# Token mixers with the written order kept on three engines, and half a stream block between bursts of the chains

## The chip, the cores and the metric

The kernel runs on one core of one Trainium2 chip. The metric is device time in microseconds (us) of one execution; three runs of the kernel before gave 1572.19, 1572.81 and 1575.52, with a median of 1572.81.

## The reference

Two layers of a decoder trunk on 256 tokens of width 1024. A layer is four steps, each followed by a layer norm of (a times x plus the step's result): a SwiGLU block of width 2816, a step of three parallel token mixers, a second SwiGLU block, and a gated embedding. The change is in the mixer step:

```python
h  = x @ W_in        # columns split among RWKV-7, GLA, gated delta rule and merge gates
x  = LN(a*x + W_o(sum_b sigmoid(h_gate_b) * (Mixer_b(h_b) @ W_branch_b)))
```

RWKV-7 (8 heads of 64) and the gated delta rule (4 heads of 128) are recurrences that are computed in chunks of 64 or 128 tokens, each with the inverse of a triangular matrix; GLA (4 heads, keys of 64, values of 128) is a gated linear attention. Each mixer ends in a norm over its heads and a gate.

## The kernel before

**Tiling.** All 256 tokens are held on chip; activations lie with channels on the 128 partitions. Products of model width are made to nearly full precision out of three matmuls: an operand is split into a rounded part, `hi`, and the rest, `lo` (`split`, L313), and hi x hi, hi x lo and lo x hi are added up. Weights come from DRAM as units of 128 x 2048, in two halves of 128 x 1024: a DMA on the queue of SyncE (SP) brings a half into `raw` (four buffers), ScalarE (ACT) casts it to `hi`, VectorE (DVE) subtracts to get `lo` (four buffers each, `ahead`, L320). `unit` (L348) hands out the next unit in the order of `plan` (L67).

**The stream.** `stream` (L681) makes the columns of the combined projection, block by block in the order of `MIX` (L55). A block of 256 columns (`col_block`, L426, tile `cb`) is 2 x 24 matmuls of 128x256, 24 for each half of its columns, into one PSUM bank; ACT and DVE then take it out: a mix with the token before (`shift_mix`, L758), a convolution of four taps (`conv`, L765), a plain copy to DRAM for the merge gates (`put`, L773). C_R, C_K and C_V are RWKV's inputs, C_LQ and C_LV GLA's, C_DQ, C_DK and C_DV the delta rule's, each of two blocks; a pair (b, h) is half h of the merge gate of branch b; ("w", b, h) is the projection of branch b to half h (`project`, L1436, tile `pj`), which needs the whole branch. The last one is left to `merge` (L1479).

**The chains.** `rwkv` (L889), `gdn` (L1168) and `gla` (L1326) are generators, as `stream` is. What stands between two of a generator's yields is one burst: often a few matmuls, and the ACT and DVE work on their result. A chain's main parts are its gates and norms, products within chunks, the inverse (`inverse`, L784: a run of small DVE operations of growing size, then three rounds of matmuls), the steps from chunk to chunk and the norm at the end (`rwkv_out`, L1090; `rms_out`, L1121). GLA goes through seven levels of products (`LEVELS`, L59).

**What sets the order.** `mixers` (L670) takes a letter at a time from `ORDER` (L57): S, R, D or L lets the stream, RWKV, the delta rule or GLA run to its next yield. That is the order in which instructions are written down. It isn't the order in which they run: a scheduler orders each engine's instructions by readiness and priority while the program is built, with weight loads and their casts at high priority (L325), and the engines then keep that order. Only where `self.hold` is set does an instruction of PE, DVE or ACT keep its written place (`Engine`, L213, `pin`, L294): in `tok_pair`, the end of `ffn`, `merge` and `ple`, and here around eight matmuls of `gram` (L984 to 988).

**PSUM.** `ps` (L302) gives a tile a bank by a label: A has four, F and G two each; `TAGS` (L27) overrides the label written at the call.

Of the kernel before, what the change touches and what calls it, by code (L numbers as in the profile page):

```python
# [19 lines left out]
F32 = mybir.dt.float32  # L20
# [5 lines left out]
RAW, HL, N4, LEAD, FIN = 4, 4, 25, (3, 3), 1  # L26
TAGS = {"ab": "A", "gcol": "A", "gih": "G", "gks": "G", "ktr": "F", "lc": "F", "lo": "A", "misc": "G", "pa": "G", "pg": "G", "pj0": "A", "pj1": "A", "pq": "A", "pw": "G", "rih": "G", "st0": "A", "st1": "G", "un": "F"}  # L27
PJ = 0
MG = (4, 5)
MO = (3, 3)  # L30
P = 128
T = 256
NT = 2
# [201 lines left out]
class Trunk:  # L235
    def __init__(self, ctx, tc, I, out, dbg=None):
# [4 lines left out]
        self.halves = [(n, q) for n, u in enumerate(self.plan) for q in range(1 if u[0] == "fmisc" else 2)]  # L241
        self.at, self.used, self.ready, self.later, self.low, self.pending = 0, 0, [], [], [], ()
        self.branch = {}
        pool = lambda name, bufs, **kw: ctx.enter_context(tc.tile_pool(name=name, bufs=bufs, **kw))
# [103 lines left out]
    def unit(self, *key):  # L348

        assert self.plan[self.used] == key, (self.plan[self.used], key)  # L350
        self.used += 1
        self.subtract()
        n = 1 if key[0] == "fmisc" else 2
        self.ahead(n - len(self.ready))
        parts = [self.ready.pop(0) for _ in range(n)]

        def part(a, n):
            q, o = divmod(a, 1024)
            return parts[q][0][:, o:o + n], parts[q][1][:, o:o + n]

        return part
# [5 lines left out]

    def tok_unit(self, pss, unit, k0, start, stop, x=None):

        xh, xl = x or (self.xh, self.xl)  # L370
        for q in range(2):
# [298 lines left out]
    def mixers(self, i):  # L670

        self.got, self.branch, self.over = {}, {}, set()
        self.maker = {"b0": "R", "b1": "L", "b2": "D"}
        self.threads = {"S": self.stream(i), "R": self.rwkv(i), "D": self.gdn(i), "L": self.gla(i)}
        for name in ORDER + "RDLS":
            self.step(name)
        for name in "RDLS":
            while name not in self.over:
                self.step(name)

    def stream(self, i):  # L681

        nc = self.nc
        A = nc.scalar
        ps = self.col_block(self.unit("fwa", i))
        wa = self.pt.tile([P, T], F32, tag="wa", name="wa", bufs=1)
# [10 lines left out]
        self.shift_mix(mx, ps[:, :T], 14)  # L697
        ab = self.pt.tile([P, NT, 8], F32, tag="ab", name="ab", bufs=1)
        ps = self.ps("ab", "G")
        for t in range(NT):  # L700
            nc.tensor.transpose(ps[:, 8 * t:8 * t + 8], mx[64:72, t * P:t * P + P], self.ident[64:72, 64:72])
        A.copy(ab[:, :, 0:4], ps[:, :16].rearrange("p (t c) -> p t c", c=8)[:, :, 0:4])
        A.activation(ab[:, :, 4:8], ps[:, :16].rearrange("p (t c) -> p t c", c=8)[:, :, 4:8], AF.Sigmoid)
# [3 lines left out]
        self.got["misc"] = gl, ab  # L707
        yield
        for item in MIX:
            if isinstance(item, tuple) and item[0] == "w":  # L710
                yield "b%d" % item[1]
                self.project(i, *item[1:])
                if item != MIX[-1]:
                    yield
            elif isinstance(item, tuple):
                d = self.pd.tile([P, D], F32, tag="gd", name="gd", bufs=8)
                for u in range(2):
                    ps = self.col_block(self.unit("fcol", i, C_MG + item[0] * D + item[1] * 512 + 256 * u))
                    self.put(ps, d, u, AF.Copy)
# [3 lines left out]
            elif item == C_LV:  # L723
                pss = [self.ps(f"st{t}", "F") for t in range(NT)]
                for u in range(2):
                    self.tok_unit(pss, self.unit("tok", i, item, u), 4 * u, u == 0, u == 1)
                    if u == 0:
                        yield
                vt = self.s4("lv").rearrange("p (t c) -> p t c", t=2)
# [4 lines left out]
            elif item == C_LQ:  # L734
                qk = self.s4("lqk")
                q, k = qk[:, :512], qk[:, 512:]
                A.activation(q, self.col_block(self.unit("fcol", i, C_LQ)), AF.Identity, scale=0.125)
                yield
                A.copy(k, self.col_block(self.unit("fcol", i, C_LK)))
                self.got[item] = q, k  # L740
                yield
            else:
                out = self.s4("c%d" % item)
                for u in range(2):
                    ps = self.col_block(self.unit("fcol", i, item + 256 * u))
                    for c in range(2):
# [142 lines left out]
    def rwkv(self, i):  # L889
# [200 lines left out]
    def rwkv_out(self, t, y, bv, gl):  # L1090
# [59 lines left out]
    def unit_norms(self, xs):  # L1150
# [3 lines left out]
        for x, _ in xs:  # L1154
            sq = self.s4("usq")
            nc.scalar.activation(sq, x, AF.Square)
            sqs.append(sq)
        for sq in sqs:
            for q in range(2):
                ps = self.ps("un", "G")  # L1160
                s = slice(q * 512, q * 512 + 512)
# [6 lines left out]
    def gdn(self, i):  # L1168
# [10 lines left out]
        yield "misc"  # L1179
        ab = self.got["misc"][1]  # L1180
        e, s, s2, q, x = (small(n) for n in ("e", "s", "s2", "q", "x"))
# [21 lines left out]
        tri = kc[:, K_INCL:K_INCL + P]  # L1203
        pg = self.ps("gcol", "G")
        self.mm(pg[:, :8], tri, x.rearrange("p t h -> p (t h)"))
# [9 lines left out]
        for t in range(NT):  # L1215
            grow = self.ps("grow", "G").rearrange("p (h c) -> p h c", c=P)
            for h in range(4):
# [12 lines left out]
        k, q = self.got[C_DK], self.got[C_DQ]  # L1230
        self.unit_norms([(k, 1.0), (q, float(P) ** -0.5)])
        yield
# [6 lines left out]
        for t in range(NT):  # L1239
            pk, pq = self.ps("pk", "G"), self.ps("pq", "G")  # L1240
            for h in range(4):
# [52 lines left out]
        for t in range(NT):  # L1294
# [11 lines left out]
            V.tensor_tensor(out=vn, in0=pv, in1=self.head_bc(beta[:, t], P), op=ALU.mult)  # L1306
            yield
            if not t:
                vd = h3(self.s2("gvd"))
                V.tensor_tensor(out=vd, in0=vn, in1=self.head_bc(ec, P), op=ALU.mult)  # L1310
                pd = h3(self.ps("gd"))
# [3 lines left out]
                yield  # L1315
            ops = self.ps("go")
# [9 lines left out]
    def gla(self, i):  # L1326
# [48 lines left out]

        lw = None
        for n, s in enumerate(LEVELS):
            v5 = lambda ap: ap.rearrange("p (m f s) -> p m f s", f=2, s=s)
            if n % 2 == 0:
# [12 lines left out]
            V.tensor_tensor(out=v5(w)[:, :, 1], in0=v5(w)[:, :, 1], in1=v5(q)[:, :, 1], op=ALU.mult)  # L1392
            grams(w, w, 1 + n, s)
            yield
        grams(k, q, 0, 0)
        yield

# [11 lines left out]
        V.tensor_tensor(out=w4[:, :, 0:2], in0=w4[:, :, 0:2], in1=k4[:, :, 0:2], op=ALU.mult)  # L1409
        V.tensor_tensor(out=w4[:, :, 2:4], in0=w4[:, :, 2:4], in1=q4[:, :, 2:4], op=ALU.mult)  # L1410
        cross = self.s4("lcross").rearrange("p (a c) -> p a c", c=P)
        pss = [self.ps("lc", "G") for _ in range(2)]
# [23 lines left out]
    def project(self, i, b, h):  # L1436
# [39 lines left out]
        half(0)  # L1476
        half(1)

# [185 lines left out]
```

## Time and profile before

| | us |
|---|---|
| median of three runs | 1572.81 |
| the profiled execution | 1568.71 |
| its span, first to last instruction | 1566.9 |
| PE / DVE / ACT / POOL busy | 1494.9 / 1058.5 / 873.3 / 49.1 |
| mean granted clock of PE, share of full speed | 0.981 |

PE is TensorE, POOL is GpSimd. Spans are counted from the first instruction. Matmuls are pipelined, so a matmul's counted time overlaps that of its successor, and a busy PE isn't a PE at its peak. In the rows, `out<-in` are tiles by the program's names (`cb` a block's bank, `pj` a projection's, `hi` and `lo` weights, `lw`, `latt` and `lg` GLA's, `rig`, `riab`, `riof` the inverse of RWKV, `sq` and `kk` its keys), then come the shapes, a count, the busy time and the mean length of one in ns, and after the second bar the idle time of the engine just before, with what ended it.

### The profile page before, as it was taken

What the parts mean: (1) busy time and instruction counts of PE and PEld (TensorE: products, weight loads), DVE (VectorE), ACT (ScalarE), POOL (GpSimd) and SP (SyncE); (2) the same over time, 40 slices, a digit from 0 to 9 for tenths busy, and PEclk for the clock granted to TensorE, in tenths of its full rate; (3) what the DMA queues carried; (4) which work ended last, traced back from release to release, by engine and by line L of the source; (5) the groups of instructions that cost most, each with busy time, mean ns of one, the idle gap of its engine ahead of it and who ended that gap; (6) DMA issues with size and microseconds to landing.
All of it is one profiled execution on the core that took longest, in us unless ns stands there. A gap on an engine that the chain in (4) does not pass through costs nothing. (4 is left out here: it accounts for less than half of the span.)

```text
span 1566.9 us, 27601 instructions
## 1 busy us (share of the span) xinstructions
PE 1494.9 (95%) x11280; PEld 1356.7 (87%) x11280; DVE 1058.5 (68%) x1597; ACT 873.3 (56%) x1229; POOL 49.1 (3%) x85
## 2 busy tenths in 40 slices
PE   8999999988998999999999999998989889999997
PEld 7999889887987989998789997897979879899986
DVE  5555757787975875556865557577789658745567
ACT  5544558856654554445654445587665555644453
POOL 0000000000002000000000000000000020000001
PEclk9999999989999999999999999999999999999999
DMA  7765655532424655656555666554425256656562
GB/s 257 264 215 189 216 190 161 169 127 80 151 84 168 233 184 177 223 189 216 177 180 192 216 189 194 195 170 153 136 75 156 82 200 219 188 170 222 189 217 81
DMA packets 79775, 277.96 MB, mean 177 GB/s; under 512 B 9376, under 2 KB 9760, under 8 KB 79648
## 3 DMA queue, kind: packets, MB, share of 16 engines
q1 hardware_dynamic: 75744, 262.76, 51.8%
q0 software_dynamic: 3616, 13.11, 2.2%
q8 instruction: 88, 1.44, 0.4%
q10 hardware_dynamic: 288, 0.33, 0.1%
q14 instruction: 39, 0.32, 0.1%
HBM read 264.63 MB, written 11.53 MB: 176 GB/s over the span
## 5 line engine op out<-in xcount | busy, mean ns | idle before, releaser
L223 DVE TENSOR_TENSOR lo<-raw,hi 128x1024 fp32r<-128x1024 f32 (+1 forms) x459 | 555.4, 1220 | 316.1 <-ACT hi L223 313.7
L223 ACT CAST hi<-raw 128x1024 fp32r<-128x1024 f32 (+1 forms) x459 | 474.9, 1047 | 430.1 <-PE h L223 144.1
L223 PE MATMUL h<-xh,hi 128*128 128x256 f32 x1088 | 306.2, 282 | 5.9 <-ACT hi L223 5.5
L223 PE MATMUL h<-xl,hi 128*128 128x256 f32 x1088 | 305.8, 281 | 0.8 <-DVE xl L223 0.8
L223 PE MATMUL h<-xh,lo 128*128 128x256 f32 x1088 | 305.4, 281 | 0.0
L223 PE MATMUL cb<-xh,hi 128*128 128x256 f32 x864 | 247.1, 286 | 14.4 <-DVE c L223 11.1
L223 PE MATMUL cb<-xl,hi 128*128 128x256 f32 x864 | 244.5, 283 | 0.0
L223 PE MATMUL cb<-xh,lo 128*128 128x256 f32 x864 | 243.4, 282 | 0.0
L223 PEld LDWEIGHTS h<-xh,hi 128*128 128x128 f32 x1088 | 204.9, 189 | 7.3 <-ACT hi L223 5.5
L223 PEld LDWEIGHTS h<-xh,lo 128*128 128x128 f32 x1088 | 208.6, 192 | 0.1
L223 PEld LDWEIGHTS h<-xl,hi 128*128 128x128 f32 x1088 | 205.1, 189 | 2.2 <-DVE xl L223 1.0
L223 PEld LDWEIGHTS cb<-xh,hi 128*128 128x128 f32 x864 | 164.7, 191 | 18.8 <-DVE c L223 11.3
L223 PEld LDWEIGHTS cb<-xl,hi 128*128 128x128 f32 x864 | 164.8, 191 | 2.4 <-issue 1.0
L223 PEld LDWEIGHTS cb<-xh,lo 128*128 128x128 f32 x864 | 164.7, 191 | 1.9 <-issue 1.0
L223 PE MATMUL y<-hi,gh 128*128 128x512 f32 x352 | 137.8, 391 | 0.0
L223 PE MATMUL y<-lo,gh 128*128 128x512 f32 x352 | 137.1, 389 | 0.0
L223 PE MATMUL y<-hi,gl 128*128 128x512 f32 x352 | 136.2, 390 | 0.3 <-DVE gl L223 0.3
L223 PE MATMUL tb<-hi,xl 128*128 128x512 f32 x224 | 87.6, 391 | 2.1 <-DVE xl L223 2.1
L223 PE MATMUL tb<-hi,xh 128*128 128x512 f32 x224 | 88.5, 395 | 0.0
L223 PE MATMUL tb<-lo,xh 128*128 128x512 f32 x224 | 88.0, 393 | 0.0
L223 PEld LDWEIGHTS y<-hi,gl 128*128 128x128 f32 x352 | 66.1, 188 | 14.7 <-DVE gl L223 0.8
L223 PEld LDWEIGHTS y<-lo,gh 128*128 128x128 f32 x352 | 66.1, 188 | 12.2
(354 smaller groups left out, 2264.0 us busy)
## 6 DMA issues: line engine op xcount, KB each, us to landing
raw<-in_ws_dram SPq DMA_DIRECT2D x457, 512.0 KB, 4.4
gb<-in_ln_dram SPq DMA_DIRECT2D x16, 512.0 KB, 6.1
gd<-sg SPq DMA_DIRECT2D x32, 256.0 KB, 4.2
sgate<-gd POOLq DMA_DIRECT2D x12, 512.0 KB, 5.8
xd<-x POOLq DMA_DIRECT2D x4, 512.0 KB, 5.8
x<-xd POOLq DMA_DIRECT2D x4, 512.0 KB, 9.0
sw<-in_sw_dram SPq DMA_DIRECT2D x2, 768.0 KB, 8.7
xt<-in_xt_dram SPq DMA_DIRECT2D x4, 256.0 KB, 5.4
```

The costliest lines, as they stand in the source:

```text
L223: ins = f(*args, **kw)
```

## The change

`mixers` sets `self.hold` for the whole step, so that every instruction of PE, DVE and ACT keeps its written place there, and a new flag, `eager`, with which `unit` at once loads, casts and subtracts the next unit. The stream yields after half a block. `MIX` and `ORDER` are new: R's keys come first, GLA's inputs earlier, the projections of GLA stand before the last two gate blocks. The chains get a few yields more, so that a matmul and the ACT work that it needs lie in two bursts; GLA's products come one level later than the work that feeds them; two transposes move from the stream to the delta rule; tiles of PSUM get other labels. The instructions are the same.

```diff
-TAGS = {"ab": "A", "gcol": "A", "gih": "G", "gks": "G", "ktr": "F", "lc": "F", "lo": "A", "misc": "G", "pa": "G", ...
+TAGS = {"gk": "G", "lc": "G", "lg": "G", "lo": "G", "misc": "F", "pg": "G", "pj0": "F", "pj1": "F", "st0": "F", "st1": "F",
+        "tp": "G"}
...
-MIX = (C_R, C_K, C_DK, C_LV, (0, 0), C_V, C_LQ, (0, 1), C_DQ, (2, 0), (1, 1), C_DV, (2, 1), (1, 0), ("w", 0, 0),
-       ("w", 1, 1), ("w", 0, 1), ("w", 1, 0), ("w", 2, 0), ("w", 2, 1))
-ORDER = ("RRSRSSSDSSRSRRSSSRRRRRRRRRRSSRSRRRSDRRRRRSRSRDRRRRRRRRDRDSDRLDRRDRDLRDDSDSSSLDLDRLRDRRRDRDDRRRDLRLDD"
-         "SDDDDSDLLSDDDLLRDLSDLLRRLLDSSDSDSLLSSSSDSLDS")
+MIX = (C_K, C_R, (2, 0), C_LQ, (2, 1), C_DK, C_DQ, (1, 0), C_V, C_LV, (1, 1), C_DV, ("w", 1, 0), ("w", 1, 1), (0, 0), (0, 1),
+       ("w", 0, 0), ("w", 0, 1), ("w", 2, 0), ("w", 2, 1))
+ORDER = ("SSSRRSRDLSSDSRSSRSRSRSRSRSSRSRSRSSLSRSLSRSLSRLSRSRLSRSRLSRSRSRDSSSRSRSRDLSSRRSRDLRSRDLRSDLSRDLRS"
+         "DSDLLSRDLRSDLLLSRDLSRDSRDLSRDSRDRSRDSRDSRDRRSRDSRDRRSDSRSRDRSRDDSRDSRDDSRDSRDRDSDSDSSSS")
...
     def unit(self, *key):
         parts = [self.ready.pop(0) for _ in range(n)]
+        if self.eager:
+            self.ahead(2 - len(self.ready))
...
     def col_block(self, unit):
             for k in range(8):
                 self.col_mm(ps[:, c * T:c * T + T], unit, k, c)
+            if not c:
+                yield
...
     def mixers(self, i):
+        self.hold = self.eager = True
         for name in ORDER + "RDLS":
             self.step(name)
...
+        self.hold = self.eager = False
...
     def rwkv(self, i):
         A.activation(sq, kk, AF.Square)
+        yield
...
-                self.hold = True
                 for n in range(4):
...
-                self.hold = False
...
     def gla(self, i):
         for n, s in enumerate(LEVELS):
+            if n:
+                grams(*last)
...
-            grams(w, w, 1 + n, s)
+            last = w, w, 1 + n, s
             yield
+        grams(*last)
+        yield
...
     def project(self, i, b, h):
         half(0)
+        yield
         half(1)
```

More yields of the same kind stand before the norm's matmul in `rwkv_out` and `unit_norms`, before GLA's cross term (`lc`), in the value block of the stream (four parts in place of two) and in the delta rule's first state step, where one yield goes.

## Rows read from the trace of the kernel before

**Rows 1.** Head and first section of the page: span, and busy time by engine
```profile
span 1566.9 us, 27601 instructions
...
PE 1494.9 (95%) x11280; PEld 1356.7 (87%) x11280; DVE 1058.5 (68%) x1597; ACT 873.3 (56%) x1229; POOL 49.1 (3%) x85
```

**Rows 2.** Table of stretches: both mixer stages; columns as in the first line
```profile
core 0: us, PE busy (x) PEld busy (x) DVE busy (x) ACT busy (x) POOL busy (x), PEclk, DMA share, GB/s
...
217.00:501.40 284.40, 261.08 (x2545) 238.43 (x2543) 213.54 (x399) 187.84 (x282) 10.06 (x19) 0.96 0.41 132
...
996.40:1280.40 284.00, 258.39 (x2541) 236.00 (x2539) 213.04 (x398) 187.88 (x282) 9.28 (x17) 0.97 0.41 132
```

**Rows 3.** Table of stretches of 20 us, layer 0, same columns
```profile
300.00:320.00 20.00, 12.64 (x106) 10.98 (x105) 19.59 (x35) 8.70 (x18) 0.00 (x0) 0.81 0.32 105
...
480.00:500.00 20.00, 14.63 (x150) 13.52 (x149) 11.08 (x24) 12.31 (x16) 3.11 (x4) 1.00 0.41 143
```

**Rows 4.** Timeline of TensorE: start, length, instruction; then tile pj's own stretch
```profile
389.61 0.28 PE L223 MATMUL cb<-xh,lo 128*128 128x256 f32 x1
...
390.29 0.28 PE L223 MATMUL cb<-xh,lo 128*128 128x256 f32 x1
...
501.41 0.79 PE L223 MATMUL pj<-bh,hi 128*128 128x256 f32 x2 [6.02 <-ACT bh L223]
...
507.09 0.28 PE L223 MATMUL pj<-bh,lo 128*128 128x256 f32 x1
...
507.21 0.28 PE L223 MATMUL pj<-bh,hi 128*128 128x256 f32 x1
...
501.40:507.00 5.60, 4.23 (x18) 4.01 (x19) 0.00 (x0) 0.50 0.77 277
```

**Rows 5.** Groups of ScalarE instructions, shapes apart, 217 to 501 us
```profile
L223 ACT CAST hi<-raw 128x1024 fp32r<-128x1024 f32 x59 | 61.0, 1049 | 43.6 <-PE cb L223 37.4 <-issue 4.7 <-DMA raw<-in_ws_dram 1.0
...
L223 ACT ACT_TABLE_LOAD x21 | 26.9, 1283 | 1.2 <-DVE c L223 0.8
...
L223 ACT ACTIVATE c<-cb,om 128x256 f32<-128x256 f32 x12 | 5.5, 474 | 4.0 <-DVE c L223 3.9
...
L223 ACT ACTIVATE sq<-av,om,cv 128x256 f32<-128x256 f32 x4 | 2.2, 593 | 0.0
```

**Rows 6.** Groups of VectorE instructions, 217 to 501 us
```profile
L223 DVE TENSOR_TENSOR lo<-raw,hi 128x1024 fp32r<-128x1024 f32 x60 | 72.5, 1219 | 22.5 <-ACT hi L223 21.6 <-PE cb L223 0.3
...
L223 DVE SCALAR_TENSOR_TENSOR c<-cb,cv,c 128x255 f32<-128x255 f32 (+2 forms) x48 | 22.7, 477 | 2.5 <-ACT c L223 1.9
...
L223 DVE COPY_PREDICATED latt<-masks,lg 128x256 f32<-128x256 uint8 (+1 forms) x16 | 7.9, 553 | 2.2 <-PE lg L223 2.2
...
L223 DVE TENSOR_TENSOR lw<-lw,lqk 128x256 f32<-128x256 f32 x16 | 6.1, 421 | 0.0
...
L223 DVE TENSOR_TENSOR rig<-gram,kc 32x256 f32<-32x256 f32 x8 | 4.7, 590 | 0.1
```

**Rows 7.** Timeline of ScalarE around one change of table
```profile
267.19 0.69 ACT L223 ACTIVATE sq<-l,eps 128x512 f32<-128x512 f32 x1 [0.17 <-PE l L223]
...
267.90 1.28 ACT L223 ACT_TABLE_LOAD   x1
...
269.20 1.06 ACT L223 ACTIVATE sq<-sq 128x1024 f32<-128x1024 f32 x1
```

**Rows 8.** Timeline of VectorE inside the inverse of RWKV, layer 0
```profile
318.87 0.70 DVE L223 STREAM_TRANSPOSE rigt<-rig 128x512 f32<-128x512 f32 x1
...
323.49 0.22 DVE L223 TENSOR_REDUCE riab<-rigt 128x8 f32<-128x64 f32 x1
...
327.41 2.35 DVE L223 TENSOR_TENSOR riof<-gram,kc 128x1024 f32<-128x1024 f32 x2
```

**Rows 9.** Waits of the DMA issuing queue SP, 217 to 545 us; page's DMA issues
```profile
SPq L329 <- DVE lo L223: 217.5, 59, 27.4
...
sgate<-gd POOLq DMA_DIRECT2D x12, 512.0 KB, 5.8
```

More of the change, by code (lines that the diff above doesn't have):

```diff
@@ L242, in __init__ @@
         self.at, self.used, self.ready, self.later, self.low, self.pending = 0, 0, [], [], [], ()
+        self.eager = False
         self.branch = {}
@@ L366, in mm3, with tok_unit @@
         self.mm(out, ll, rh, False, stop)
-    def tok_unit(self, pss, unit, k0, start, stop, x=None):
+    def tok_unit(self, pss, unit, k0, start, stop, x=None, qs=range(2)):
         xh, xl = x or (self.xh, self.xl)
-        for q in range(2):
+        for q in qs:
             for t in range(NT):
@@ L684, in stream @@
         A = nc.scalar
-        ps = self.col_block(self.unit("fwa", i))
+        ps = yield from self.col_block(self.unit("fwa", i))
         wa = self.pt.tile([P, T], F32, tag="wa", name="wa", bufs=1)
@@ L697, in stream @@
         self.shift_mix(mx, ps[:, :T], 14)
[L698 to L703, printed above, removed]
         nc.gpsimd.memset(gl[:, 1:], 0.0)
@@ L706, in stream @@
         A.copy(gl[32:48, 2], mx[32:48])
-        self.got["misc"] = gl, ab
+        self.got["misc"] = gl, mx
         yield
@@ L711, in stream @@
                 yield "b%d" % item[1]
-                self.project(i, *item[1:])
+                yield from self.project(i, *item[1:])
                 if item != MIX[-1]:
@@ L717, in stream @@
                 for u in range(2):
-                    ps = self.col_block(self.unit("fcol", i, C_MG + item[0] * D + item[1] * 512 + 256 * u))
+                    ps = yield from self.col_block(self.unit("fcol", i, C_MG + item[0] * D + item[1] * 512 + 256 * u))
                     self.put(ps, d, u, AF.Copy)
@@ L725, in stream @@
                 for u in range(2):
-                    self.tok_unit(pss, self.unit("tok", i, item, u), 4 * u, u == 0, u == 1)
-                    if u == 0:
-                        yield
+                    un = self.unit("tok", i, item, u)
+                    for q in range(2):
+                        self.tok_unit(pss, un, 4 * u, u == 0, u == 1, qs=(q,))
+                        if (u, q) != (1, 1):
+                            yield
                 vt = self.s4("lv").rearrange("p (t c) -> p t c", t=2)
@@ L736, in stream @@
                 q, k = qk[:, :512], qk[:, 512:]
-                A.activation(q, self.col_block(self.unit("fcol", i, C_LQ)), AF.Identity, scale=0.125)
+                ps = yield from self.col_block(self.unit("fcol", i, C_LQ))
+                A.activation(q, ps, AF.Identity, scale=0.125)
                 yield
-                A.copy(k, self.col_block(self.unit("fcol", i, C_LK)))
+                ps = yield from self.col_block(self.unit("fcol", i, C_LK))
+                A.copy(k, ps)
                 self.got[item] = q, k
@@ L744, in stream @@
                 for u in range(2):
-                    ps = self.col_block(self.unit("fcol", i, item + 256 * u))
+                    ps = yield from self.col_block(self.unit("fcol", i, item + 256 * u))
                     for c in range(2):
@@ L1157, in unit_norms @@
             sqs.append(sq)
+        yield
         for sq in sqs:
             for q in range(2):
-                ps = self.ps("un", "G")
+                ps = self.ps("un")
                 s = slice(q * 512, q * 512 + 512)
@@ L1179, in gdn @@
         yield "misc"
-        ab = self.got["misc"][1]
+        mx = self.got["misc"][1]
+        ab = self.pt.tile([P, NT, 8], F32, tag="ab", name="ab", bufs=1)
+        ps = self.ps("ab")
+        for t in range(NT):
+            nc.tensor.transpose(ps[:, 8 * t:8 * t + 8], mx[64:72, t * P:t * P + P], self.ident[64:72, 64:72])
+        A.copy(ab[:, :, 0:4], ps[:, :16].rearrange("p (t c) -> p t c", c=8)[:, :, 0:4])
+        A.activation(ab[:, :, 4:8], ps[:, :16].rearrange("p (t c) -> p t c", c=8)[:, :, 4:8], AF.Sigmoid)
         e, s, s2, q, x = (small(n) for n in ("e", "s", "s2", "q", "x"))
@@ L1203, in gdn @@
         tri = kc[:, K_INCL:K_INCL + P]
[L1204 removed]
+        pg = self.ps("gcol")
         self.mm(pg[:, :8], tri, x.rearrange("p t h -> p (t h)"))
@@ L1230, in gdn @@
         k, q = self.got[C_DK], self.got[C_DQ]
-        self.unit_norms([(k, 1.0), (q, float(P) ** -0.5)])
+        yield from self.unit_norms([(k, 1.0), (q, float(P) ** -0.5)])
         yield
@@ L1310, in gdn @@
                 V.tensor_tensor(out=vd, in0=vn, in1=self.head_bc(ec, P), op=ALU.mult)
+            yield
+            if not t:
                 pd = h3(self.ps("gd"))
@@ L1374, in grams @@
                     "p (a b s) -> p a b s", a=4, s=out.shape[3]))
-        lw = None
+        lw = last = None
         for n, s in enumerate(LEVELS):
+            if n:
+                grams(*last)
             v5 = lambda ap: ap.rearrange("p (m f s) -> p m f s", f=2, s=s)
@@ L1476, in project @@
         half(0)
+        yield
         half(1)
```

10 lines of the change are left out of this document (4 added, 6 removed).

## The prediction

> **What bounds the kernel now.** I read the head of the page first: the span is 1566.9 us and PE counts as busy for 95% of it [rows 1]. Its profiled execution took 1568.7, 1.8 around the span. The three runs have a median of 1572.8, 4.1 above it; I sum against the profile and add 4.1 at the end.
>
> The change touches the mixers alone, once a layer. The table of stretches, cut from the first matmul of the first block to the first of a branch projection, gives 284.4 in layer 0 and 284.0 in layer 1, with PE busy 261.1 and 258.4, DVE 213.5, ACT 187.8 [rows 2]. So PE visibly idles for 23.3 in layer 0, in a few places: 7.4 of it in one 20 us slice where DVE is busy 19.6 and the granted clock falls to 0.81, 5.4 in the last slice, where the chains run out [rows 3]. After that the projections stand alone: the first waits 6.0 for ACT and starts at half clock, 18 matmuls in 5.6 us, then one each 0.12 [rows 4]. Five of the six projections (240 matmuls; the sixth belongs to the merge) take 5.6 + 222 x 0.12 = 32.2. **The stage with its five projections is 284.4 + 32.2 = 316.6 us**; that is the number to beat, twice.
>
> Busy PE hides waits. A block's matmuls start every 0.113 us (0.68 for six) but each counts 0.28 [rows 4], so a wait under 0.17 is not seen as idle.
>
> **What the change does, part by part.** It takes nothing out and adds nothing but order: 54 half blocks, 59 bursts of R, 34 of D, 20 of L, the same instructions. PE's own work, with no wait: a half block is 24 x 0.114 = 2.73; 54 of them are 147.4, the small block and the value block 14, five projections 28.8. The chains' bursts I take at 75, from the spacing of their matmuls; they lie between that and 261.1 - 161 = 100, which busy time leaves and which holds the hidden waits. Sum 265.3. So the waits of PE in the new order may come to 316.6 - 265.3 = **51.3 a layer before the kernel is slower**.
>
> Removed: the scheduler's choice on PE, DVE and ACT. Today it can put a weight subtraction of 1.22 [rows 6] between any two operations of a chain, once its cast is there. Added: each engine takes its instructions as written. A block's weights are cast on ACT (2 x 1.05) and subtracted on DVE (2 x 1.22) one block ahead, at the head of the block before [rows 5, 6]. The cover is that block, 2 x 2.73 = 5.5 of PE, and any chain work that ACT or DVE has in front of the casts eats it: 5.5 - 2.1 - 1.2 leaves 2.2. I walked the new order slot by slot: an engine starts an instruction when it is free and the last input is there, durations from the groups, two in a row overlapping by about 0.09 (two products of 1.22 in 2.35 [rows 8]), 0.05 allowed for a hand-over. The waits of PE that come out, per layer:
>
> - **Opening, 25.7**: the decay projection behind seven ACT steps 3.6, the cumulative gate 1.5, R0 3.3, the l2 sum behind ACT's copies 4.5, R1 2.5, (2,0)1 6.1, LQ 3.4, (2,1)0 0.9. One in full, (2,0)1: after the casts of the block before, ACT has a table load 1.28, an exponential 1.06, a wait for a DVE product 1.22, four scalings of 0.59, R1's two copies 0.95, three exponentials 3.18, then its casts 2.10 and the subtraction 1.22 [rows 5 to 7]: 13.4. PE has left of R1 and both halves of (2,0)0 7.3. Wait 6.1.
> - **Middle, 24.4**: DQ0 0.5, a GLA level 1.9, DQ1 3.1, (1,0)0 8.7, (1,0)1 6.2, the inverse's product 3.2, the cross term 0.9. In full, (1,0)0, on DVE: four mask products 0.59, a GLA step of two predicated copies 0.53 and four of 0.42 with ACT's exponential between them 0.7, six convolution taps 0.48, the first part of the inverse from 318.87 to 323.71 = 4.84, two subtractions 2.44 [rows 6, 8]: 15.8, less 1.6 of overlap, 14.2, against 5.5 of PE. Wait 8.7.
> - **Late, 13.8**: GLA's transposes behind DVE 3.9, (1,1)0 and (1,1)1 2.8, the delta inverse 3.5, the state steps of RWKV 3.6 in four.
> - **End, 5.9**: the branch b0 behind its norm, 5.5, where the present kernel waits 6.0, and b2 0.3.
>
> Sum 69.8; 59.8 of it in fifteen waits of 1.9 or more. The ten small ones (10.0) sit within the error of walking whole bursts, where an instruction may need only the first matmul: from 0 to 10.0, and I take half. **Stage 265.3 + 64.8 = 330.1, 13.5 longer; two layers 27.0; 1568.7 + 27.0 = 1595.7, and 4.1 for the median: 1599.8.**
>
> Edits at nothing: the transposes of a and b move to D and stay two; the GLA products move one level later; new yields issue nothing. New bank labels: any wait of that kind today is inside PE's 23.3 of idle time; from 0 to that, taken 0, since the stream keeps two banks and R and D four. SP: its weight loads lose their priority but wait 217 us for free buffers now [rows 9], and four buffers hold two blocks; taken 0. POOL: gates come back in 5.8 [rows 9], and in order ACT's sigmoid in front of the next casts would wait for that; from 0 (POOL ran ahead) to 5 x (5.8 - 2.2) = 18 a layer, taken 0 because POOL is busy 10 of 284 [rows 2]. Clock: a slice in which it fell shows 0.81 [rows 3], 0.19 x 20 = 3.8 of full speed lost. The walk has ten waits over 3, today's stage some four falls; from 0 to 6 x 3.8 = 23, taken 0 because the waits are spread out between dense blocks.
>
> Table loads: I count 20 changes of function set against 21 [rows 5]. Between the logarithm's end at 267.88 and the exponential's start at 269.20 lies the load of 1.28 and 0.04 more [rows 7], so a change costs 1.3. The Trainium skill, "ScalarE: Activation LUTs", section "What ACT_TABLE_LOAD costs", adds a drain of about 1.38 to each load; the trace does not show one. By the page six loads in the opening would add an estimated 8.3 a layer to ACT there, and the sum would be some 1616; as no row shows the drain, this gets no chance of its own.
>
> **Rivals.** *Faster: the casts are not late.* Its place is the queue of ACT and DVE in front of the stream's own blocks: ten of the waits (R0, R1, (2,0)1, LQ, (2,1)0, DQ0, DQ1, (1,0)0, (1,0)1, (1,1)1) are casts that stand behind bursts, 36.5 a layer. If bursts are shorter than I charge them, these go, the stage is 265.3 + 33.3 = 298.6, 18.0 shorter, and the time 1572.8 - 36 = 1537. It decides where 18.5 of the 36.5 go (13.5 if half the small waits go too). For it: ACT now idles 37.4 before casts, waiting only for PE to free a buffer [rows 5], so capacity is there, and the order has empty slots after heavy bursts. Against it: that idle time is spread over the stage, and the opening's ACT steps are long ones in a row.
>
> *No change: about half of them go*, waits near 51.3, within 1.6 a layer. The present kernel hides some 24.6 (261.1 - 236.5) behind busy matmuls and idles 23.3, so a trade of one kind of wait for another is possible. That the order is the old one in effect is excluded: blocks and projections change places.
>
> *Slower by more: the clock and the gates.* Ten waits over 3 us pull the clock down as they do now, 23, or ACT waits for gates, 18, a layer. With half of both, 41 over two layers, the time is 1600 + 41 = 1641. For it: PE's slices with 12.6 of 20 busy run at 0.81 [rows 3]. Against: most waits end within one block's length.
>
> **How the numbers follow.** The forecast, slower by one to three per cent, gets 0.57: the opening and the middle are sums of long instructions that must pass one queue. Faster gets 0.25, since the walk is coarse and its margin, 13.5 of 330, is small; no change 0.08; slower by more 0.10. Faster or slower by 0.2%, 3.1 us, is about what a measurement of this kernel tells from no change. The forecast's own range is 1590 (no small wait) to 1625 (all waits, 1610, and a third of the clock's bound, 15). The range for eight in ten goes from 1548, which leaves out about half of the faster case, to 1628, which leaves out most of the last one.
>
> **What would show it.** Right: DVE and ACT alternate in bursts, the group of casts shows idle before cb blocks on PE released by DVE lo, 25 or so in the first 90 us of a stage and again around the first inverse; the 6.0 before the projections stays near 5.5, and stage and projections take about 330. Wrong: PE idle below 23 a stage and hardly any before cb released by lo (the casts are on time, the faster rival); or slices at 0.8 clock in many more places (the third); or ACT waiting for the DMA of sgate. The forecast falls as a whole if ACT's casts stand ahead of bursts that are written before them.

## The result, and the profile after

The changed kernel takes **1690.74 us** (median of four executions, 1688.28 to 1693.27) against 1572.94 for the kernel before beside it: a ratio of **1.0746, with an interval of 1.0725 to 1.0767**. That is 118 us slower; forecast were 27, and the upper end of the range was 1628.

First the head of the page after, then its table of stretches: from the first block to the first projection in both layers, and, in layer 0, on to the end of the fifth projection.

```profile
span 1688.1 us, 27535 instructions
...
PE 1534.0 (91%) x11280; PEld 1387.5 (82%) x11280; DVE 1068.6 (63%) x1597; ACT 859.3 (51%) x1220; POOL 49.2 (3%) x85
```
```profile
core 0: us, PE busy (x) PEld busy (x) DVE busy (x) ACT busy (x) POOL busy (x), PEclk, DMA share, GB/s
218.50:493.60 275.10, 224.57 (x1985) 203.54 (x1983) 188.73 (x346) 150.45 (x231) 6.11 (x13) 0.88 0.34 115
1057.30:1333.20 275.90, 224.21 (x1986) 204.96 (x1984) 188.81 (x346) 150.63 (x231) 6.13 (x13) 0.89 0.35 115
218.50:587.20 368.70, 307.98 (x2793) 282.51 (x2792) 242.20 (x429) 199.13 (x297) 12.73 (x24) 0.89 0.37 125
```

DVE and ACT do nearly the work that they did [rows 1]; PE counts as busy for 39 us more with the same matmuls, so they took longer one by one. **The stage with five projections is 368.7 us in layer 0 and 369.7 in layer 1, against 316.7 in both before**: 105 together, of the 121 by which the two profiled spans differ. The merge's last product, behind it, grew from 23.8 to 29.5 and from 23.8 to 29.3, another 11. No other stretch grew by over 2.5. The projections are now spread among the gate blocks, so the first 275 us are not the same work as [rows 2]; only whole stages compare.

In stretches of 20 us, the picture that before showed in a few slices [rows 3] is now the rule in the first half of the stage: clock 0.83, PE short of work, and no single engine full.

```profile
220.00:240.00 20.00, 16.10 (x95) 12.22 (x93) 5.99 (x7) 12.05 (x22) 0.00 (x0) 0.83 0.31 106
...
280.00:300.00 20.00, 13.84 (x91) 12.93 (x90) 10.47 (x11) 16.42 (x24) 0.00 (x0) 0.83 0.26 90
300.00:320.00 20.00, 20.00 (x187) 19.48 (x187) 14.14 (x21) 13.65 (x22) 0.00 (x0) 1.00 0.68 233
...
360.00:380.00 20.00, 10.54 (x74) 9.90 (x72) 17.02 (x48) 4.19 (x7) 0.00 (x0) 0.74 0.23 82
380.00:400.00 20.00, 13.92 (x84) 11.40 (x84) 12.30 (x17) 16.02 (x21) 0.00 (x0) 0.83 0.38 132
```

What takes turns there shows best in the view of waits (who waits for what, us in total, times, longest). ACT and DVE waiting for each other in a stage, before:

```profile
DVE lo L223 <- ACT hi L223: 22.6, 18, 4.6
...
ACT c L223 <- DVE c L223: 10.5, 8, 3.5
ACT lw L223 <- DVE lw L223: 7.6, 2, 5.6
...
DVE c L223 <- ACT c L223: 1.9, 3, 0.8
```

and after (217 to 587 us):

```profile
DVE lo L224 <- ACT hi L224: 60.3, 24, 10.7
...
ACT lw L224 <- DVE lw L224: 34.7, 8, 13.3
ACT c L224 <- DVE c L224: 29.5, 14, 10.4
...
DVE c L224 <- ACT c L224: 15.8, 16, 4.2
```

Together 43 us before and 140 after. The groups say the same of the casts: ACT used to idle 43.6 in front of them, waiting for PE to free a buffer [rows 5], and now never does.

```profile
L224 ACT CAST hi<-raw 128x1024 fp32r<-128x1024 f32 x69 | 68.6, 1043 | 0.1
L224 ACT ACT_TABLE_LOAD x18 | 23.1, 1283 | 5.2 <-DVE c L224 4.9
```

So a cast now runs when its turn in ACT's queue comes, not when its buffer is free, and the blocks wait for its results, 10.6 for hi and 8.2 for lo in layer 0 (PE's groups, 218.5 to 587.2 us):

```profile
L224 PE MATMUL cb<-xh,hi 128*128 128x256 f32 x432 | 129.8, 301 | 15.0 <-ACT hi L224 10.6 <-DVE c L224 4.5
L224 PE MATMUL cb<-xh,lo 128*128 128x256 f32 x432 | 125.2, 290 | 8.2 <-DVE lo L224 8.2
```

One such turn in the timelines, PE, then ACT, then DVE, around (1,0)0 and (1,0)1, the two blocks of the gate (1, 0):

```profile
367.35 0.55 PE L224 MATMUL cb<-xh,hi 128*128 128x256 f32 x1 [4.46 <-DVE c L224]
...
373.13 0.58 PE L224 MATMUL cb<-xh,lo 128*128 128x256 f32 x1 [5.01 <-DVE lo L224]
...
385.65 0.58 PE L224 MATMUL cb<-xh,hi 128*128 128x256 f32 x1 [5.62 <-ACT hi L224]
```
```profile
355.05 1.98 ACT L224 CAST hi<-raw 128x1024 fp32r<-128x1024 f32 x2
357.05 1.28 ACT L224 ACT_TABLE_LOAD   x1
362.30 0.63 ACT L224 ACTIVATE lw<-lw 128x512 f32<-128x512 f32 x1 [3.97 <-DVE lw L224]
...
365.55 1.98 ACT L224 CAST hi<-raw 128x1024 fp32r<-128x1024 f32 x2
```
```profile
356.12 2.36 DVE L224 TENSOR_TENSOR lo<-raw,hi 128x1024 fp32r<-128x1024 f32 x2 [1.10 <-ACT hi L224]
358.39 2.44 DVE L224 TENSOR_TENSOR rig<-gram,kc 32x256 f32<-32x256 f32 x4
360.84 0.77 DVE L224 COPY_PREDICATED latt<-masks,lg 128x256 f32<-128x256 uint8 x2
361.51 0.75 DVE L224 TENSOR_TENSOR lw<-lxb 128x256 f32<-128x256 f32 x2
...
367.12 0.70 DVE L224 STREAM_TRANSPOSE rigt<-rig 128x512 f32<-128x512 f32 x1
...
371.86 2.35 DVE L224 TENSOR_TENSOR lo<-raw,hi 128x1024 fp32r<-128x1024 f32 x2
```

DVE waits 1.10 for the casts, then does its subtractions, the mask products and GLA's step; ACT, which has the next casts behind GLA's exponential, stands 3.97 for that; the casts follow at 365.55 and end at 367.5; but in DVE's order the first part of the inverse, a row of small operations from 367.12 on, stands in front of the subtractions, and they come at 371.86. PE waits 4.46 for a bank that the convolution still reads and 5.01 for lo. No wait is long, and each is handed on.

### The profile page after: what moved, and what is told of

Same layout as the page of the kernel before. It is cut to its first block, busy times and chain, and to the rows that moved or that the text cites. A ratio compares the mean times of both kernels' runs of the same rounds, so it can differ in the third digit from the quotient of the medians.

```text
span 1688.1 us, 27535 instructions
## 1 busy us (share of the span) xinstructions
PE 1534.0 (91%) x11280; PEld 1387.5 (82%) x11280; DVE 1068.6 (63%) x1597; ACT 859.3 (51%) x1220; POOL 49.2 (3%) x85
## 4 chain that ended last, share of the span: by engine, by line
PE 57%; DVE 21%; ACT 12%; DMA 5%; issue 4%; POOL 1%; SPq 0%; POOLq 0%; DVEq 0%; ACTq 0%
PE h L224 22%; PE y L224 11%; PE cb L224 7%; PE tb L224 6%; DVE lo L224 5%; DMA raw<-in_ws_dram 4%; ACT hi L224 4%; DVE c L224 3%; PE pj L224 2%; ACT L224 2%; PE wo L224 2%; DVE z L224 1%; ACT c L224 1%; DVE lw L224 1%; PE tp L224 1%
## 5 line engine op out<-in xcount | busy, mean ns | idle before, releaser
L224 ACT CAST hi<-raw 128x1024 fp32r<-128x1024 f32 (+1 forms) x459 | 468.8, 1045 | 307.1 <-PE h L224 146.2
L224 PE MATMUL cb<-xh,hi 128*128 128x256 f32 x864 | 260.7, 302 | 32.3 <-ACT hi L224 23.4
L224 PE MATMUL cb<-xh,lo 128*128 128x256 f32 x864 | 251.4, 291 | 16.4 <-DVE lo L224 16.4
L224 PE MATMUL cb<-xl,hi 128*128 128x256 f32 x864 | 250.2, 290 | 0.0
L224 PEld LDWEIGHTS cb<-xh,hi 128*128 128x128 f32 x864 | 174.0, 201 | 37.7 <-ACT hi L224 33.8
L224 PEld LDWEIGHTS cb<-xh,lo 128*128 128x128 f32 x864 | 172.9, 200 | 19.5 <-DVE lo L224 19.4
L224 PEld LDWEIGHTS cb<-xl,hi 128*128 128x128 f32 x864 | 173.7, 201 | 2.4 <-issue 2.0
```

Of the source, the lines that this page charges most:

```text
L224: ins = f(*args, **kw)
```

## The experiments

In each run the figure in brackets is the difference to the kernel before on the same chip (1573.89, 1580.13, 1573.87, 1574.07 and 1574.89 in the five sets: one execution, in the third set the median of eleven); each changed kernel but the last two ran once, and differences under some 8 us are not read. The products computed are the same in all; only the fillers of the clock test add matmuls, whose result nothing reads.

**Which part.** The new layout without the pins (hold and eager loading off in `mixers`, the hold around `gram` back):

```diff
-        self.hold = self.eager = True
+        self.hold = self.eager = False
```


> The new kernel with its order, its half blocks, its bursts and its PSUM labels, but hold and eager off in the mixers (and on again around the eight gram matmuls, as before), so that the scheduler orders PE, DVE and ACT. Theory Q (the written order in the queues is what costs; the layout is harmless): within 1% of the kernel before, 1557 to 1589, with some four stretches at half clock per mixer stage. Theory L (the new order of blocks and projections is worse by itself): above 1640.

Measured 1589.79 (+15.9), stages of 320.9 and 321.5: theory Q, less than 1 us above its range. The layout costs some 16; the pins cost about 100. The old layout with the pins:

> The kernel before, with its old MIX, ORDER, labels and bursts, but hold and eager on over the whole mixer step. Q: pinning costs whatever the layout, and the old order has runs of up to ten bursts of one chain in a row and whole blocks between, so it is slower than the new kernel, above 1750. L: the old layout is the better one, so pinned it stays below 1640.

Measured 1869.66 (+295.8). The new order is far better to pin than the old one, which was never meant to be run as written. Then the pins on one kind of engine, the rest left to the scheduler:

```diff
-            return self.trunk.pin(ins) if self.trunk.hold else ins
+            hold = self.trunk.hold and (not self.trunk.eager or self.tag in "P")
+            return self.trunk.pin(ins) if hold else ins
```


> The new kernel with the written order kept on PE only; DVE and ACT are ordered by the scheduler in the mixers. Q in its narrow form (casts and subtractions stand behind bursts in ACT's and DVE's queues): PE's waits before stream blocks for hi, lo and c (some 24 of 60 us a layer) go, the waits before chain matmuls stay in part: 1600 to 1645. Theory P (it is PE's own order that waits for late bursts while stream matmuls were ready): 1670 or more.

> The new kernel with the written order kept on DVE and ACT only; PE is ordered by the scheduler in the mixers. Narrow Q: most of the loss stays, 1650 or more. P: most of it goes, below 1620.

PE alone pinned: 1630.52 (+56.6). DVE and ACT alone: 1705.72 (+131.8), more than all three. Both are narrow Q's, but with PE alone pinned only the waits of blocks for hi and lo are gone; 19.0 a stage are left in front of them for banks. With DVE and ACT in written order, a free PE gains nothing.

**The clock.** Dummy matmuls in front of the waits, so that PE is busy while it waits:

```diff
+    def fill(self, n):
+        ps = self.ps("fill")
+        for _ in range(n):
+            self.mm(ps[:, :T], self.xh[:, 0, :P], self.xh[:, 0])
...
+        self.fill({6: 38, 7: 4, 15: 40, 16: 46}.get(n, 0))
         ps = self.ps("cb", "F")
```


> The new kernel, with dummy matmuls of 128x256 (some 470 a layer, 4 to 46 at a place) written on TensorE in front of fifteen of the places where it now waits, each set worked out to last about as long as the wait (0.113 us each); they read the held activations and write a spare PSUM tile that nobody reads. The real instructions and their order are those of the new kernel. Theory K (the waits come out as walked, and the rest of the loss is the clock that falls behind them: 82 and 78 us a layer at half clock against 31 and 24 before): visible idle time falls under 30 a layer, half-clock time under 40 in at most 6 stretches, the stage is 335 to 350 and the time 1625 to 1655. Rival W (the clock falls cost nothing of their own, for the other engines set the pace and TensorE would only wait longer at full clock): half-clock time falls too, but the time is 1680 to 1710.

Measured 1677.41 (+97.3); stages of 360.2 and 364.0. To read it, I cut a stage (layer 0) by the starts in PE's timeline: a matmul is charged the time to the next start, without the idle time in front of that, and goes to the level of clock granted there.

| us | stage | matmuls at 2.4 GHz | at 1.2 GHz | fillers | idle | at 2.4 GHz throughout | stretches at 1.2 GHz |
|---|---|---|---|---|---|---|---|
| before | 316.7 | 270.9 | 22.5 | | 23.3 | 282.2 | 4, 30.7 |
| layout only | 320.9 | 270.3 | 23.2 | | 27.4 | 281.9 | 5, 27.3 |
| after | 368.7 | 247.7 | 60.2 | | 60.7 | 277.8 | 12, 81.9 |
| after, filled | 360.2 | 272.4 | 12.5 | 54.6 | 20.6 | 278.7 | 3, 13.7 |
| after, casts and subtractions free | 344.9 | 265.9 | 27.2 | | 51.8 | 279.5 | 7, 41.0 |

The row of the filled stage, with a clock of 0.98 in place of 0.89:

```profile
216.40:576.60 360.20, 339.60 (x3230) 317.59 (x3229) 241.54 (x429) 199.32 (x297) 12.74 (x24) 0.98 0.37 126
```

The half clock costs 30.1 of PE's time in a stage after (half of 60.2) and 6.3 when filled; but of the 23.8 that this gives back, 14.5 go into longer waits (54.6 + 20.6 = 75.2 against 60.7) and only 8.5 of the stage is won. Theory K's signs came, its price didn't, and 1677.41 lies just under rival W's range: for the most part a slow PE used up time in which it would have waited for DVE and ACT. Fillers can also overrun. In three places of layer 0, in front of (1,0)0, inside it and in front of (1,0)1, the matmul behind them starts without a wait; of the first two they overran some 2.7 and 1.8. But the third follows casts that begin at 379.82, a first one of 1.04, and starts at 381.08. DVE, on which those casts hang, had no idle time from 362.33 on, so what was overrun only shortened that wait. In layer 1 the filled stage is 364.0, with 23.9 at 1.2 GHz, and only 6 are won.

**Casts and subtractions.** Both given back to the scheduler, everything else pinned (`held` saves the flag, which is set back behind):

```diff
     def ahead(self, n, wide=False, defer=False, pieces=1):
+        held, self.hold = self.hold, self.hold and not self.eager
```


> The new kernel, with everything pinned as there except the weights' casts on ScalarE and their subtractions on VectorE, which get back the scheduler's choice and the high priority that they have before. Theory C (the casts stand in line behind long bursts, which is the largest part of the loss; the chains' own work in written order costs less): the waits of the first matmul of a block on hi or lo, some 28 a layer with their falls of the clock, go nearly all; time 1600 to 1645. Rival O (it is the chains' own operations, taken strictly as written, that are late; the casts only show it): waits move to the chains' tiles and the time is over 1665.

Measured 1633.19 (+53.1), as theory C has it: 65 of the 118 go (58 by the two times themselves; the kernel before took 1580.13 on this chip). The stages are 344.9 and 346.0. Blocks no longer wait for lo (0.9 in a stage, 8.2 pinned) or hi; what is left in front of them is banks not yet emptied.

```profile
L224 PE MATMUL cb<-xh,hi 128*128 128x256 f32 x432 | 126.2, 292 | 12.6 <-ACT c L224 7.4 <-DVE c L224 2.9 <-ACT sg L224 1.5
L224 PE MATMUL cb<-xh,lo 128*128 128x256 f32 x432 | 121.3, 281 | 0.9 <-DVE lo L224 0.9
```
```profile
DVE lo L224 <- ACT hi L224: 29.0, 26, 3.9
...
ACT c L224 <- DVE c L224: 24.6, 12, 4.3
...
ACT lw L224 <- DVE lw L224: 15.3, 4, 8.5
...
DVE c L224 <- ACT c L224: 6.3, 9, 2.3
```

(First fence PE's groups, second its waits.) The four mutual waits sum to 75 in place of 140. In a stage 68 of the 69 casts and 59 of the 69 subtractions now stand earlier in their queue, none later. Then one of the two at a time: the same two lines put around the subtractions in `subtract`, or around the cast in `ahead`.

> The new kernel, everything pinned but the subtractions on VectorE, which the scheduler may place, with their priority; the casts on ScalarE keep their written places. Theory T: this alone gives most of the 58 us that freeing casts and subtractions together gave: 1630 to 1660 (against 1580 for the kernel before on that chip). Rival A (the late place is that of the casts on ScalarE, behind tables and exponentials; VectorE only shows it): 1668 or more.

> The new kernel, everything pinned but the weights' casts on ScalarE, which the scheduler may place; the subtractions on VectorE keep their written places. In the instruction order that results, many pairs of casts stand a few instructions later in ScalarE's queue than written (behind a chain's copies or a table load), some a few earlier (ahead of an eviction). Theory A (ScalarE's queue is where the loss arises): the same as with both freed, 1615 to 1650. Rival T (casts and subtractions have to move together): 1665 or more.

Subtractions free: 1684.99 (+111.1), the mutual waits those of the changed kernel to 0.1. Casts free: 1666.67 (+92.6). That is 7, too small to be read, and 25; both together gave 65. In order, DVE's idle time in front of lo with the subtractions free and with the casts free, and PE's with the casts free:

```profile
L224 DVE TENSOR_TENSOR lo<-raw,hi 128x1024 fp32r<-128x1024 f32 x69 | 81.6, 1221 | 60.3 <-ACT hi L224 60.2
```
```profile
L224 DVE TENSOR_TENSOR lo<-raw,hi 128x1024 fp32r<-128x1024 f32 x74 | 87.2, 1218 | 6.2 <-ACT hi L224 5.8
```
```profile
L224 PE MATMUL cb<-xh,lo 128*128 128x256 f32 x432 | 124.3, 288 | 13.0 <-DVE lo L224 13.0
```

The first run tests little. `ahead` asks for the high priority only where `hold` is off, which it isn't there, so the subtractions are without the priority that the expectation gives them, and only 10 of 69 in a stage change their place. One of them is that of (1,0)0: its wait for lo, 5.01, is gone, and the next, for hi in front of (1,0)1, is 9.53 where it was 5.62. In the second run 67 of 69 casts stand earlier in ACT's queue, by 4.5 instructions on average (the expectation has many of them later); with both free it is 68, by the same 4.5. So what sets these two runs apart is mainly where the subtractions stand. DVE's waiting for casts goes with the casts alone, but a subtraction in its written place still stands among the chain's work, and PE's waits for lo stay. The stages, 352.0 and 359.5, are 7 and 14 longer than with both free; the rest lies outside them. The four mutual waits, though, sum to 70 there, no more than with both free: their sum does not tell the time. Next the written place itself. Later subtractions, behind half a block and a burst:

```diff
-            self.ahead(2 - len(self.ready))
+            self.ahead(2 - len(self.ready), defer=True)
...
             if not c:
                 yield
+                self.subtract()
```


> The new kernel, everything pinned, with one thing moved: the weights' casts stay at the head of a block, but the two subtractions on VectorE are written after the block's first half and the chain burst that follows it. Theory T (taking turns: with the subtraction at the head, VectorE stands 60 us of a stage in front of it for a cast that is late in ScalarE's queue, the chains' VectorE work behind it starts late, and ScalarE in turn waits for that): idle time of VectorE before lo falls below 35 a layer and the time to 1635 to 1675. Rival M (the order of the two only moves the wait: lo is then late for TensorE): the waits of the first matmul of a block on lo grow by what the others lose, time over 1682.

Measured 1729.26 (+155.4): rival M. DVE's idle time in front of lo fell from 60.3 to 17.6, and PE paid most of it back, 47.3 a stage in front of lo, from 8.2. Part of that is the edit: behind a unit that isn't a block (GLA's values, a projection) the subtractions come only at the head of the unit that uses them, and 8.9 of the 47.3, in front of (1,1)0, are of that kind, with 11 more in front of values and projections. The four mutual waits sum to 101 here, less than the 140 of the faster changed kernel.

```profile
L224 PE MATMUL cb<-xh,lo 128*128 128x256 f32 x432 | 129.2, 299 | 47.3 <-DVE lo L224 47.3
```

And earlier casts, right behind the block's last matmul:

```diff
                 yield
+        self.ahead(4 - len(self.ready))
         return ps
```


> The new kernel, everything pinned, with casts and subtractions written one eviction and one chain burst earlier: right behind the last matmul of the block before, in place of the head of the next block. Theory L (the casts are late for the stream, because bursts stand in front of them): the waits of a block's first matmul on hi and lo shrink, 1640 to 1675. Rival H (both engines then stand at the head of their queue for TensorE to give back the buffers of the block that it has just finished, and the chains' bursts behind them are late instead): 1690 or more.

Measured 1706.15 (+132.1), 14 slower than the change as it stands: rival H's side. In the timeline the waits for hi go and come back as waits for banks that the convolution hasn't emptied and for the inverse, as rival H's second half says; its first half is small, ACT idles only 5.3 in front of casts for PE. **Moving casts and subtractions one burst earlier, or subtractions later, makes it worse; letting the scheduler place both, with their priority, wins 65.** That the burst is too coarse a unit for them is the likely reason; no run writes them at a finer one.

**TensorE's order.** Free DVE and ACT, and on PE only the stream's matmuls pinned, or only the chains' (`now` is the letter that runs):

```diff
-            hold = self.trunk.hold and (not self.trunk.eager or self.tag in "P")
+            hold = self.trunk.hold and (not self.trunk.eager or self.tag in "P" and (self.trunk.now == "S") is True)
```


> The new layout, VectorE and ScalarE free in the mixers as in the kernel before, and on TensorE only the stream's matmuls kept in written order (among themselves and against nothing else); the chains' matmuls are free. Theory S (a block that is not ready holds up the queue, since nothing of the stream may pass it): 1610 to 1635, near the 1630 of TensorE wholly pinned. Rival C (it is the chains' places that cost): 1585 to 1602, near the layout without pins.

> The counterpart: VectorE and ScalarE free, on TensorE only the chains' matmuls kept in written order, the stream's free. Theory S: 1585 to 1605. Rival C: 1615 to 1635. If both stay under 1605, it is the order between stream and chains, not within one of them, that costs.

Measured 1608.55 (+33.7) and 1589.53 (+14.6). The first lies between the two theories, a little under S, the second in S's range. Against the layout without pins (+15.9), the chains' order costs nothing, the stream's some 18; both pinned together cost 41. The 23 left over would be the order between them, if these costs add up; the scheduler also orders DVE and ACT anew in each of these runs, so that isn't shown.

**One wait taken away.** GLA's two gate matmuls before the reads of their bank; the pinned kernel shows 5.17 in front of the second, which the prediction's walk had passed over.

```diff
             self.mm(ps[:, s], self.sw[:, 1024 + c * P:1024 + c * P + P], misc)
+        for c in range(2):
+            s = slice(c * T, c * T + T)
             A.activation(x[:, s], ps[:, s], AF.Identity, ...
```


> The new kernel, everything pinned, with one change: GLA's two gate matmuls stand before the two ScalarE reads of their bank, so that the second doesn't wait for the first read. Theory G (each wait that TensorE shows is paid): 4 to 6 us a layer go, 1678 to 1684. Rival F (in the opening another engine's queue sets the pace, and the wait moves to the next place where TensorE needs ScalarE): 1687 to 1695, with the wait in front of the l2 sum or of the next block longer by as much.

Measured 1693.96 (+119.1): nothing won. The wait is gone and the next ones are longer: the l2 sum 4.81 where it was 3.16, the block (2,0)1 5.74 where it was 4.31, and 2.17 in front of the cumulative gate, which had none: 5.25 in all. The l2 sum, in the changed kernel and then without the gate's wait:

```profile
267.60 3.78 PE L224 MATMUL l<-sq,kc 128*128 128x512 f32 x4 [3.16 <-ACT sq L224]
```
```profile
267.89 3.47 PE L224 MATMUL l<-sq,kc 128*128 128x512 f32 x4 [4.81 <-ACT sq L224]
```

**Two attempts at a faster kernel**, both the kernel before, unpinned, with one idea each: GLA's last bursts earlier and its projections first; the delta rule's blocks in other banks.

```diff
-MIX = (C_R, C_K, C_DK, C_LV, (0, 0), C_V, C_LQ, (0, 1), C_DQ, (2, 0), (1, 1), C_DV, (2, 1), (1, 0), ("w", 0, 0),
-       ("w", 1, 1), ("w", 0, 1), ("w", 1, 0), ("w", 2, 0), ("w", 2, 1))
+MIX = (C_R, C_K, C_DK, C_LV, (0, 0), C_V, C_LQ, (0, 1), C_DQ, (2, 0), (1, 1), C_DV, (2, 1), (1, 0), ("w", 1, 0),
+       ("w", 1, 1), ("w", 0, 0), ("w", 0, 1), ("w", 2, 0), ("w", 2, 1))
...
-         "SDDDDSDLLSDDDLLRDLSDLLRRLLDSSDSDSLLSSSSDSLDS")
+         "SDDDDSDLLSDDDLLRDLSLDLLRRLLDLSSDSDSLSSSSDSDS")
```


> The kernel before, unpinned as it is, with two edits taken from the new layout's idea: GLA's last three bursts are written 3 to 10 letters earlier, and the stream projects branch b1 before b0, so that TensorE has projections while RWKV's norm ends. Theory E (the 6.0 us in front of the projections and the half clock after it are paid on the path): 4 to 8 us a layer go, 1556 to 1566. Rival N (the scheduler moves the same wait to another place, all three chains ending together): within 4 us of the kernel before.


```diff
-                    ps = self.col_block(self.unit("fcol", i, item + 256 * u))
+                    ps = self.col_block(self.unit("fcol", i, item + 256 * u), "A" if item in (C_DQ, C_DK, C_DV) else "F")
```


> The kernel before, unpinned, with the blocks of the delta rule that go through the convolution in the four banks of label A in place of the two of label F. Theory E (TensorE's 5.4 us in front of a block at 318.6, with 10 us of half clock around it, is a bank that the convolution holds): 4 to 8 us a layer go, 1557 to 1567. Rival N (the chains then wait for the banks of A, or the scheduler orders them after one another): 1570 or more.

The first is 1578.76, a ratio of 1.0034 (1.0015 to 1.0052), 4.9 slower and so a little outside rival N's 4: the 6.02 in front of the projections [rows 4] is now 5.68 in front of GLA's transposes,

```profile
500.82 0.45 PE L223 MATMUL tp<-kc,mo 128*128 128x128 f32 x1 [5.68 <-DVE mo L223]
```

which fits rival N's reason, that the chains end together and it matters little which branch is projected first. The second is 1615.83, 1.0263 (1.0243 to 1.0283): the wait at the block fell from 5.4 to 4.1, and new ones of 6.8 (inverse behind ACT) and 7.9 (a transpose behind ACT) came. No version here beats the kernel before.

## Why the prediction was wrong

The sign was right. **What failed are three terms of the sum, PE's own work (265.3; it measured 277.8), its waits with the small ones halved (64.8; 75 at full clock) and the clock (0), and the merge, which wasn't in it.** Stage 330.1 was forecast and 368.7 came; the table of stages gives the 38.6 as 12.5 of own work, 30.1 of half clock, less 4.1 of waits (60.7 against 64.8). That the visible waits come so near to 64.8 is partly luck, since the slow clock uses up waits. The filled stage takes the clock apart from them: its 360.2 are 30.1 over the forecast, 13.4 of own work, 10.4 of waits and 6.3 of half clock that is left; the other 8.5 are what keeping the clock up won. Two layers at 38.6 and 39.6, and 11.2 in the merge, make 89; 1599.8 + 89 = 1689.

- **PE's own work.** I took a run's spacing, 0.114 a matmul, for all 54 half blocks. By the starts, a matmul followed by another of a block takes 0.1187 on average in the kernel before (40 of 1236 take over 0.15), one before a change from block to chain 0.19, at the median 0.21, and the value block's 48 take 0.24 each, nearly as the prediction has it: 170 to 171 for the blocks in place of 161. The kernel before's own stage, at full clock, is 282.2 (blocks 170.5, chains 83 where I took 75, projections 28.7), so it held 34.5 of waits and slow clock, not 51.3. In the new order the blocks take 171, the chains 77 and the projections 29.5, so 75 was near and the blocks are what was too low. The limit at which the change turns slower was 17 too high by the old order's work, 12 by the new one's. This work still holds waits too short to show as idle. The check that shows it, 316.7 less idle time less clock loss, could have been made on the kernel before.
- **The clock.** The bound was right, 0 to 23 a layer: PE's loss at half clock grew by 18.8 in layer 0 (30.1 - 11.3) and by 21.7 in layer 1. Taking 0 "because the waits are spread out between dense blocks" was wrong: 12 and 13 stretches at 1.2 GHz came in place of 4 and 4, about as many as there are waits over 2.5. But these 19 to 22 are not what the clock costs: with it kept up the stage is only 6 to 8.5 shorter, though some half clock is left there.
- **The waits at full clock** are then 75 (table, filled), where the walk had 69.8 and I took 64.8: halving the small ones was wrong, and the walk missed the gate matmul (5.2) and underrated GLA's transposes (5.3 for 3.9). Places, walked and measured: opening 25.7 and 18.4, middle 24.4 and 22.2, late 13.8 and 11.5, end 5.9 and 7.9; in the filled stage, fillers counted as waits, they are 24.6, 26.7, 14.8 and 9.2. (1,0)0, worked in full as 8.7 (its terms add up to 16.0, not 15.8), came as 9.5, but half of it for the bank, which the walk did not have there; (2,0)1, 6.1, came as 4.8.
- **Edits at nothing.** SP: casts idle 0.1, so the loads are in time. Bank labels: blocks wait 4.5 for banks, 5.4 before. POOL: ACT waits once a stage for a gate, 6.1, and one projection 2.8 behind it; 0 was too low, the bound of 18 far. The merge was not in the sum at all: behind the pinned end of the stage PE waits there 2.29 for the split of the merged halves, then 0.85 and 0.47 for the weights, where it waited 0.76, and half clock adds 2.7.
- **Table loads**: 18 in the stage, not 20. One ends at 273.08 with the logarithm starting at 273.09:

```profile
271.80 1.28 ACT L224 ACT_TABLE_LOAD   x1
273.09 1.27 ACT L224 ACTIVATE sq<-l,eps 128x512 f32<-128x512 f32 x2
```

  so the extra drain that the Trainium skill, "ScalarE: Activation LUTs", section "What ACT_TABLE_LOAD costs", adds does not show after the change either. The estimate of 1616 made with it is nearer to the result, for a reason that isn't there.
- **Rivals.** Casts not late: excluded, blocks wait 18.8 a stage for hi and lo, in (2,0)1, LQ, DQ1, (1,0) and (1,1)1, half of the 36.5 walked; R0, R1, (2,1)0 and DQ0 had none. No change: the limit was never near. Slower by more, 0.10: its first mechanism, the clock falling behind each wait, came in full, its second at a third; its time, 1641, was still 50 short, since it was built on the same low 265.3 and left the longer waits out.

What the prediction lacked as a mechanism is the coupling. It charged each wait to the instructions in front of it in one queue and added them up; the runs show that a wait taken away comes back at the next place (1693.96, and (1,0)1 with the subtractions free) and that moving the casts and subtractions returns nothing (1706.15, 1729.26). That the two queues hand a delay back and forth fits the timelines, but is argued: the sum of their mutual waits fell to 101 and 70 in runs of 1729.26 and 1666.67. Some 53 us of the loss stay with casts and subtractions free; which of the chains' pinned places cost them is open.

## What to carry to other kernels

Before pinning a written order, ask which instructions are independent feeders (weight casts, subtractions, loads): written into the queues of two engines at one place each they stand behind work that isn't ready, and giving both back to the scheduler, with their priority, won 65 of 118 us here. Before reading a run in which something was set free, count how many instructions changed their place in the queue: 10 of 69 said little. Measure a stage's own work as its length less idle time less clock loss in the kernel at hand, not as a count times the best spacing. And judge a wait by what is late next: in a stage whose engines wait for each other, the one wait that was taken away gave nothing back.

## What the runs showed of the hardware

Keeping TensorE at 2.4 GHz with dummy matmuls works as far as the clock goes (0.89 to 0.98 over the stage) and costs the other engines nothing that the table shows (DVE 241.5 for 242.2, ACT 199.3 for 199.1), yet wins only 6 to 8.5 us a stage, where PE's matmuls get back 19 to 24. Here a clock fall behind a wait for other engines was mostly paid out of the next wait.

Left open: whether the 23 us on TensorE are the order between stream and chains, and whether a finer written order, with a cast or a subtraction between single steps of a burst, would reach what the scheduler reaches.
